# Stores of the split mixer weights on the queues of the engines that make them: high parts on ACT's, low parts on GpSimd's

## The chip, the cores and the metric

One NeuronCore of a Trainium2 chip. The time is the device time of one launch in microseconds (us); smaller is better. The engines are PE (TensorE), DVE (VectorE), ACT (ScalarE), POOL (GpSimd) and SP (SyncE). [...]

## The reference, cut to what matters

Two layers of a hybrid token mixer with a convolutional FFN, in fp32, over 512 latent tokens (`x`) and 256 context tokens (`ctx`), model width 1024:

```python
for l in range(DEPTH):                        # DEPTH = 2
    m_lat = split((silu(c) @ w_mod[l] + b_mod[l])[:, None, :], 6)
    m_ctx = split(silu(c_ctx) @ w_mod[l] + b_mod[l], 6)
    h_lat, h_ctx = modulate(x, m_lat[0], m_lat[1]), modulate(ctx, m_ctx[0], m_ctx[1])
    y_lat, y_ctx = token_mixer(h_lat, h_ctx, w_in[l], ..., w_out[l])
    x = layer_norm(ALPHA * x + m_lat[2] * y_lat, ...)
    f_lat = conv_ffn(modulate(x, m_lat[3], m_lat[4]), w_up[l], conv_w[l], w_down[l])
    x = layer_norm(ALPHA * x + m_lat[5] * f_lat, ...)
    if l == 0:                                # the same for ctx
        ...
def conv_ffn(h, w_up, conv_w, w_down, ...):
    u = conv3x3(h @ w_up)                     # 2 * 2816 columns, depthwise 3x3
    a, g = split(u, 2)
    return (silu(g) * a) @ w_down
```

## The kernel before, in words

**Products.** Every fp32 operand of a matmul is split into a high part `hi`, rounded to fp32r, and a low part `lo = x - hi`. A product is three matmuls: high by high (L183), high by low (L184), low by high (L185). ACT makes a high part (a copy, L147 and L164), POOL the low part (a subtraction in two halves, `sub_lo`, L133).

**The stage that the change touches** is layer 0's `ffn_up`, about 346 to 730 us in the trace. It runs over 44 column tiles of `w_up`. For each, `load` takes the weights from memory (SP, L140), splits them (ACT L147, POOL L133 into `lo`), and PE multiplies them with the latent tokens (result `ul`) and the context tokens (result `uc`), 48 matmuls in all. DVE then adds the nine taps of the convolution (`acc`, L945, behind a first tap by ACT, L916 and L918), and ACT (L948) and POOL (L949) finish a pair of tiles with `silu(g) * a` into `gT`.

**The queue of side work.** Behind each `load`, `fill(2)` takes two units from the list `queue`, so that work for layer 1 is done beside layer 0's matmuls. There are three kinds:

- `dot` (L315 to L318): a load of 512 KB of layer 1's modulation weights `wmodT`, then one multiply-and-sum pass by DVE (L318).
- `row` (L273 to L278): a load of 512 KB (`wmodR`), then four matmuls by PE (`mg`, L277).
- `split` (L159 to L170): a load of a block of layer 1's mixer weights (ten of `w_feat` and four of `w_tokB`, 512 KB each, four of `w_tokA`, 288 KB), a high part by ACT into `sh` (L164), a low part by POOL in place (`ms`, L133), and then two stores to scratch memory: the high part (`wh_f`, `wh_a`, `wh_b`, L168) and the low part (`wl_f`, `wl_a`, `wl_b`, L169). These 36 stores are what the change touches. Their data are first read back by `load_split` (L178), from about 925 us on.

The units stand in chunks of eight: dot, dot, dot, split, split, dot, row, row. All of them work in one pool of three buffers (tag `ms`); `sh` has a single buffer. So the first load of a chunk needs a buffer that the second split of the chunk before it gives back, which is when its low store has landed; and the second split's ACT pass needs the first split's high store to have landed.

**Order.** A scheduler arranges the instructions of each engine from the program and its own estimate of times. Before, both stores were issued by SP, in one stream with the loads of `w_up`, `wmodT`, `wmodR` and the mixer weights.

Of the kernel before, what the change touches and what calls it, by code (L numbers as in the profile page):

```python
# [58 lines left out]
def kernel(  # L59
# [22 lines left out]
    nc = tc.nc  # L82
# [39 lines left out]
    def hcol(k, t, n=1):  # L122
        if t < 4:
            a = slice(t * 128, (t + n) * 128)
            return hl[k][:, a], ll[k][:, a]
        a = slice((t - 4) * 128, (t - 4 + n) * 128)
        return hc[k][:, a], lc[k][:, a]

    def f(ap):
        return ap.bitcast(F32)  # L130

    def sub_lo(eng, lo, src, hi):
        eng.tensor_tensor(out=lo, in0=src, in1=f(hi), op=ALU.subtract)  # L133
# [23 lines left out]
    def split_units(srcs, ms):  # L157

        def step(key, src, n):  # L159
            st = ms.tile([128, 1024], F32, tag="ms", name="ms")  # L160
            hi = ms.tile([128, 1024], F32R, tag="sh", name="sh", bufs=1)
            d = [dram.tile([128, n], F32, name=f"w{p}_{key[0]}{key[1]}") for p in "hl"]
            nc.sync.dma_start(out=st[:, :n], in_=src)
            S.activation(out=hi[:, :n], in_=st[:, :n], func=AF.Copy)  # L164
            lo = st.bitcast(F32R)
            for a, b in ((0, n // 2), (n // 2, n)):
                sub_lo(G, lo[:, a:b], st[:, a:b], hi[:, a:b])
            nc.sync.dma_start(out=d[0], in_=f(hi[:, :n]))  # L168
            nc.sync.dma_start(out=d[1], in_=st[:, :n])  # L169
            split[key] = d  # L170

        return [lambda x=x: step(*x) for x in srcs]
# [914 lines left out]
    with tc.tile_pool(name="msA", bufs=2) as ms:  # L1087
        with tc.tile_pool(name="in0", bufs=1) as work, tc.tile_pool(name="ms0", bufs=5) as work_ms:
# [25 lines left out]
            for k in range(KT):  # L1114
# [5 lines left out]
                for v, (t0, n) in enumerate(((0, 4), (4, 2))):  # L1120
# [3 lines left out]
                    hi, lo = hcol(k, t0, n)  # L1124
# [169 lines left out]
```

## Time and profile before

| | |
|---|---|
| median of 3 runs | 1513.44 us (1511.74 to 1513.91) |
| the profiled execution | 1510.28 us |
| its span (first to last instruction) | 1508.5 us, so 1.78 us lie around it |
| mean granted clock of PE | 0.989 of full speed |
| busy: PE, DVE, POOL, ACT | 1448.1, 1172.2, 830.0, 544.7 us |

Busy time is an average over stages with different limits; the prediction reads the stage of the change by itself. In the trace "SPq" is SP's stream of DMA issues, "idle before, releaser" names what ended an engine's wait, and the chain of waits follows the work that ended last backwards, from each step to what released it.

### The profile page before, as it was taken

Reading aid. Unit: us, or ns where it says so; the run is one execution under the profiler, and the core shown is the slowest. Engines: PE = TensorE matmul, PEld = TensorE weight load, DVE = VectorE, ACT = ScalarE, POOL = GpSimd, SP = SyncE. Lnnn points to the kernel's source line nnn. Section 1 sums busy time; section 2 is a strip of 40 time slices with the busy share of each in tenths; the row PEclk is TensorE's granted clock in tenths of the full one; section 3 lists DMA queues with packets and bytes.
Section 4 is the critical chain, followed back from the end, with each engine's and each line's share of the span. In section 5 each row is a group of like instructions: output and inputs, shape, how many; then the busy total and the mean of one; then the engine's idle time right before and its main releaser. Section 6 shows DMA issues by size and latency. Waiting matters only on the chain.

```text
span 1508.5 us, 22357 instructions
## 1 busy us (share of the span) xinstructions
PE 1448.1 (96%) x8389; PEld 1185.7 (79%) x8389; DVE 1172.2 (78%) x1896; ACT 544.7 (36%) x936; POOL 830.0 (55%) x695
## 2 busy tenths in 40 slices
PE   6999999999999989999999989999899999999997
PEld 5776567788788878888888767986678888888875
DVE  6429987796988888787533699798687999889596
ACT  5443224245333322323211234254426454443121
POOL 2432635455665655543445597215466888777374
PEclk9999999999999999999999999999999999999999
DMA  9544410634877666521432366632162333333431
GB/s 377 195 165 158 140 54 15 228 135 159 313 266 240 239 215 216 178 70 56 165 100 85 116 204 239 209 125 71 58 234 72 98 98 98 98 98 93 173 112 56
DMA packets 67196, 227.11 MB, mean 151 GB/s; under 512 B 7289, under 2 KB 7945, under 8 KB 66065
## 3 DMA queue, kind: packets, MB, share of 16 engines
q1 hardware_dynamic: 67088, 225.69, 44.3%
q8 instruction: 66, 1.08, 0.3%
q14 instruction: 42, 0.34, 0.1%
HBM read 198.12 MB, written 27.55 MB: 150 GB/s over the span
## 4 chain that ended last, share of the span: by engine, by line
PE 62%; DVE 14%; DMA 12%; POOL 6%; issue 4%; ACT 2%; SPq 1%; POOLq 0%; DVEq 0%; ACTq 0%
PE ul L183 8%; PE ul L184 8%; PE ul L185 8%; PE f L187 5%; PE f L188 5%; PE f L189 5%; DMA ms<-in_wmodT 3%; POOL lo L133 2%; PE fl L183 2%; PE fl L185 2%; PE fl L184 2%; DVE acc L730 2%; DMA wl_f<-ms 2%; POOL ms L133 2%; PE tk L187 2%
## 5 line engine op out<-in xcount | busy, mean ns | idle before, releaser
L133 POOL TENSOR_TENSOR lo<-st,hi 128x512 fp32r<-128x512 f32 x300 | 412.2, 1397 | 228.0 <-ACT hi L147 175.1
L945 DVE SCALAR_TENSOR_TENSOR acc<-ul,cvw,acc 128x441 f32<-128x441 f32 (+2 forms) x660 | 437.1, 690 | 43.4 <-ACT acc L916 20.6
L147 ACT ACTIVATE hi<-st 128x1024 fp32r<-128x1024 f32 (+1 forms) x176 | 184.6, 1051 | 366.1 <-PE f L189 164.1
L184 PE MATMUL ul<-ll,hi 128*128 128x512 f32 (+1 forms) x768 | 286.4, 374 | 0.7 <-POOL ll L133 0.4
L183 PE MATMUL ul<-hl,hi 128*128 128x512 f32 (+1 forms) x768 | 284.8, 375 | 1.1 <-ACT hl L369 1.1
L185 PE MATMUL ul<-hl,lo 128*128 128x512 f32 (+1 forms) x768 | 285.4, 373 | 0.0
L187 PE MATMUL f<-hi,gh 128*128 128x512 f32 x440 | 171.8, 395 | 1.2 <-DVE gh L1007 1.2
L188 PE MATMUL f<-lo,gh 128*128 128x512 f32 x440 | 172.6, 394 | 0.0
L189 PE MATMUL f<-hi,gl 128*128 128x512 f32 x440 | 164.3, 396 | 6.4 <-POOL gl L133 5.3
L183 PEld LDWEIGHTS ul<-hl,hi 128*128 128x128 f32 x768 | 144.5, 190 | 28.3 <-issue 2.5
L185 PEld LDWEIGHTS ul<-hl,lo 128*128 128x128 f32 x768 | 145.5, 189 | 25.7 <-issue 0.4
L184 PEld LDWEIGHTS ul<-ll,hi 128*128 128x128 f32 x768 | 145.7, 190 | 24.6 <-POOL ll L133 0.7
L949 POOL TENSOR_TENSOR gT<-acc 128x768 f32<-128x768 f32 (+1 forms) x44 | 69.8, 1586 | 96.1 <-ACT acc L948 76.0
L730 DVE SCALAR_TENSOR_TENSOR acc<-cy,cmw,acc 128x798 f32<-128x798 f32 (+1 forms) x120 | 117.0, 1016 | 0.8
L183 PE MATMUL uc<-hc,hi 128*128 128x256 f32 x352 | 100.6, 286 | 6.5 <-DVE acc L945 6.4
L189 PEld LDWEIGHTS f<-hi,gl 128*128 128x128 f32 x440 | 82.6, 189 | 27.1 <-POOL gl L133 7.7
L185 PE MATMUL uc<-hc,lo 128*128 128x256 f32 x352 | 100.4, 285 | 0.0
L184 PE MATMUL uc<-lc,hi 128*128 128x256 f32 x352 | 100.4, 285 | 0.0
L187 PEld LDWEIGHTS f<-hi,gh 128*128 128x128 f32 x440 | 83.3, 189 | 20.6 <-issue 1.8
L188 PEld LDWEIGHTS f<-lo,gh 128*128 128x128 f32 x440 | 83.2, 189 | 18.3
L1007 DVE CAST gh<-gT 128x256 fp32r<-128x256 f32 x66 | 37.4, 572 | 64.9 <-PE f L188 64.9
L133 POOL TENSOR_TENSOR gl<-gT,gh 128x256 fp32r<-128x256 f32 x66 | 54.8, 833 | 57.8 <-DVE gh L1007 50.7
(304 smaller groups left out, 2843.6 us busy)
## 6 DMA issues: line engine op xcount, KB each, us to landing
st<-in_w_up SPq DMA_DIRECT2D x88, 512.0 KB, 3.5
st<-in_w_down SPq DMA_DIRECT2D x66, 512.0 KB, 3.5
ms<-in_wmodR SPq DMA_DIRECT2D x48, 512.0 KB, 4.1
ms<-in_wmodT SPq DMA_DIRECT2D x32, 512.0 KB, 3.7
ms<-in_wmod SPq DMA_DIRECT2D x8, 1024.0 KB, 12.3
st<-in_w_out SPq DMA_DIRECT2D x16, 512.0 KB, 3.5
x<-z SPq DMA_DIRECT2D x16, 512.0 KB, 2.8
z<-x SPq DMA_DIRECT2D x14, 512.0 KB, 8.8
```

The source lines that it names most:

```text
L133: eng.tensor_tensor(out=lo, in0=src, in1=f(hi), op=ALU.subtract)
L147: S.activation(out=hi[:, :n], in_=st[:, :n], func=AF.Copy)
L183: PE.matmul(ps, wh, xh, start=first, stop=False)
L184: PE.matmul(ps, wh, xl, start=False, stop=False)
L185: PE.matmul(ps, wl, xh, start=False, stop=last)
L187: PE.matmul(ps, xh, wh, start=first, stop=False)
L188: PE.matmul(ps, xh, wl, start=False, stop=False)
L189: PE.matmul(ps, xl, wh, start=False, stop=last)
L730: V.scalar_tensor_tensor(out=acc[i][:, :cw], in0=src, scalar=wj, in1=acc[i][:, :cw], op0=ALU.mult, op1=ALU.add)
L945: V.scalar_tensor_tensor(out=d, in0=u, scalar=w, in1=d, op0=ALU.mult, op1=ALU.add)
L949: G.tensor_tensor(out=gT[i][:, :n], in0=ag[:, :n], in1=aa[:, :n], op=ALU.mult)
L1007: V.tensor_copy(out=gh, in_=src)
```

## The change

The two stores of a split unit are issued by other engines. The high part's store goes from SP to ACT, the engine that made the high part; the low part's store goes from SP to GpSimd, the engine that made the low part. Nothing else differs; a blank line moves the lines behind 167 up by one.

```diff
             for a, b in ((0, n // 2), (n // 2, n)):
                 sub_lo(G, lo[:, a:b], st[:, a:b], hi[:, a:b])
-            nc.sync.dma_start(out=d[0], in_=f(hi[:, :n]))
-            nc.sync.dma_start(out=d[1], in_=st[:, :n])
+
+            nc.scalar.dma_start(out=d[0], in_=f(hi[:, :n]))
+            nc.gpsimd.dma_start(out=d[1], in_=st[:, :n])
             split[key] = d
```

What the scheduler makes of it is shown at three places. The first is POOL in the second chunk (near 403 us in the trace), where `ms` is the low part of a split unit, `lo` that of a tile of `w_up`, and `gT` the product that ends a pair of tiles. Before, with both stores on SP:

```order
L133 TENSOR_TENSOR ms<-ms,sh 128x512 x2
L133 TENSOR_TENSOR lo<-st,hi 128x512 x2
L133 TENSOR_TENSOR ms<-ms,sh 128x512 x2
L949 TENSOR_TENSOR gT_3372<-acc 128x768
L133 TENSOR_TENSOR lo<-st,hi 128x512 x4
```

And now:

```order
L133 TENSOR_TENSOR ms<-ms,sh 128x512 x2
L133 TENSOR_TENSOR lo<-st,hi 128x512 x2
L170 DMA wl_f_3906<-ms 128x1024
L133 TENSOR_TENSOR ms<-ms,sh 128x512 x2
L950 TENSOR_TENSOR gT_3372<-acc 128x768
L170 DMA wl_f_4001<-ms 128x1024
L133 TENSOR_TENSOR lo<-st,hi 128x512 x4
```

The stores of both split units now stand behind another POOL operation: the first behind two `lo`, the second, which ends the chunk, behind a `gT`.

The second place is POOL from the end of the fifth chunk to the sixth (about 489 to 528 us). Before:

```order
L133 TENSOR_TENSOR ms<-ms,sh 128x512 x4
L133 TENSOR_TENSOR lo<-st,hi 128x512 x2
L949 TENSOR_TENSOR gT_3378<-acc 128x768
L133 TENSOR_TENSOR lo<-st,hi 128x512 x4
L133 TENSOR_TENSOR ms<-ms,sh 128x288 x2
L949 TENSOR_TENSOR gT_3379<-acc 128x768
L133 TENSOR_TENSOR lo<-st,hi 128x512 x2
L133 TENSOR_TENSOR ms<-ms,sh 128x288 x2
```

And now:

```order
L170 DMA wl_f_4897<-ms 128x1024
L133 TENSOR_TENSOR ms<-ms,sh 128x512 x2
L133 TENSOR_TENSOR lo<-st,hi 128x512 x2
L170 DMA wl_f_4992<-ms 128x1024
L950 TENSOR_TENSOR gT_3378<-acc 128x768
L133 TENSOR_TENSOR lo<-st,hi 128x512 x4
L133 TENSOR_TENSOR ms<-ms,sh 128x288 x2
L950 TENSOR_TENSOR gT_3379<-acc 128x768
L170 DMA wl_a_5225<-ms 128x576
L133 TENSOR_TENSOR lo<-st,hi 128x512 x2
L133 TENSOR_TENSOR ms<-ms,sh 128x288 x2
L170 DMA wl_a_5320<-ms 128x576
```

The store that ends the fifth chunk (`wl_f_4992`) stands behind two `lo`, the first of the sixth (`wl_a_5225`) behind a `gT`, and the one that ends the sixth (`wl_a_5320`) directly behind its own subtraction.

The third place is SP in the sixth chunk (about 516 to 534 us). Before:

```order
L163 DMA ms<-in_w_tokA 128x576
L168 DMA wh_a_5224<-sh 128x576
L163 DMA ms<-in_w_tokA 128x576
L317 DMA ms<-in_wmodT 128x1024
L169 DMA wl_a_5225<-ms 128x576
L168 DMA wh_a_5319<-sh 128x576
L275 DMA ms<-in_wmodR 128x1024
L140 DMA st<-in_w_up 128x1024
L275 DMA ms<-in_wmodR 128x1024
L169 DMA wl_a_5320<-ms 128x576
L317 DMA ms<-in_wmodT 128x1024
```

And now:

```order
L163 DMA ms<-in_w_tokA 128x576 x2
L318 DMA ms<-in_wmodT 128x1024
L276 DMA ms<-in_wmodR 128x1024 x2
L140 DMA st<-in_w_up 128x1024
L318 DMA ms<-in_wmodT 128x1024
```

SP's stream keeps its loads, nearly in their old order, and no longer holds a store between them. Over the whole program 11 of the 18 low stores stand directly behind their own subtraction on POOL, and 7 behind a `gT` or two `lo`.

## Rows read from the trace of the kernel before

**Rows 1.** Busy time by stretch: us, PE, PEld, DVE, ACT, POOL, PEclk, DMA, GB/s.

```profile
380.00:390.00 10.00, 8.16 (x65) 6.68 (x58) 10.00 (x19) 2.11 (x3) 3.72 (x4) 1.00 0.94 328
...
530.00:552.00 22.00, 17.28 (x103) 14.45 (x102) 16.98 (x28) 4.80 (x8) 8.31 (x6) 0.92 0.53 174
...
576.00:730.00 154.00, 154.00 (x912) 135.31 (x911) 124.99 (x208) 50.67 (x73) 78.34 (x57) 1.00 0.37 120
348.00:730.00 382.00, 374.25 (x2254) 326.61 (x2253) 314.65 (x519) 128.23 (x189) 205.53 (x150) 0.99 0.58 194
```

**Rows 2.** Waits of PE, 350 to 660 us: total, times, longest.

```profile
PE uc L183 <- DVE acc L945: 6.4, 4, 4.0
PE mg L277 <- DMA ms<-in_wmodR: 0.6, 1, 0.6
```

**Rows 3.** The chain of waits, 400 to 580 us: start, us, what.

```profile
406.48 4.93 DMA wl_f<-ms
...
424.08 5.05 DMA wh_f<-sh
...
434.10 8.32 DMA wl_f<-ms
...
455.00 6.80 DMA wh_f<-sh
...
465.63 4.80 DMA wl_f<-ms
...
487.34 4.96 DMA wh_f<-sh
...
496.12 5.92 DMA wl_f<-ms
...
528.01 5.85 DMA wl_a<-ms
533.87 3.38 DMA ms<-in_wmodT
...
537.39 2.00 DVE ms L318 x2
...
548.94 2.77 DMA ms<-in_w_tokA
...
563.94 3.31 DMA wl_a<-ms
...
571.65 1.23 DVE ms L318 x2
...
574.01 0.35 PE uc L183
```

**Rows 4.** Waits in SP's stream, 350 to 660 us: total, times, longest.

```profile
SPq L168 <- ACT sh L164: 25.0, 12, 4.3
SPq L317 <- DMA wl_f<-ms: 17.3, 5, 7.9
...
SPq L169 <- POOL ms L133: 16.9, 14, 2.2
```

**Rows 5.** Timeline of SP's stream near 430 us: start, duration, instruction.

```profile
430.75 0.38 SPq L140 DMA_DIRECT2D st<-in_w_up  x1
432.79 0.81 SPq L275 DMA_DIRECT2D ms<-in_wmodR  x2
```

**Rows 6.** Timeline of POOL near 520 us: start, duration, instruction.

```profile
519.57 1.58 POOL L133 TENSOR_TENSOR ms<-ms,sh 128x288 fp32r<-128x288 f32 x2 [11.55 <-ACT sh L164]
521.11 1.84 POOL L949 TENSOR_TENSOR gT<-acc 128x768 f32<-128x768 f32 x1
522.91 2.55 POOL L133 TENSOR_TENSOR lo<-st,hi 128x512 fp32r<-128x512 f32 x2
```

**Rows 7.** DMA issues of two lines on SP: ns min/median/max, first and last start.

```profile
L169 SPq DMA_DIRECT2D wl_f<-ms x10: 326/326/962, 375.5 to 496.1; - x10
L140 SPq DMA_DIRECT2D st<-in_w_up x88: 327/328/1230, 278.9 to 1342.2; - x88
```

## The prediction

> **What bounds the kernel now.** I read the busy time by stretch first, since the change touches one stage only. PE is busy for 374.25 of the 382 us from 348 to 730 us [rows 1], so no more than 7.75 us of PE's idle time is there to be won. From 576 us on it is busy without a gap, 154.00 of 154.00 us: what happens to the side work after that reaches nobody. So only the stretch before 576 us can gain, and the whole stage can lose.
>
> Next, what PE waits for. Five waits hold nearly all of that idle time: four for DVE's taps, 6.4 us together, one of them 4.0 us, and one of 0.6 us for a load of `wmodR` [rows 2]. From 530 to 552 us PE was also granted only 0.92 of its clock [rows 1], which on 17.28 busy us cost about 17.28 x 0.08 = 1.4 us. So 6.4 + 0.6 + 1.4 = 8.4 us is the most that the change can take away.
>
> Then the chain of waits, to see why DVE is late [rows 3]. It is a loop through the three `ms` buffers. The low store that ends a chunk has to land (528.01 + 5.85 = 533.86 us); at 533.87 the next chunk's first `wmodT` load can start; it takes 3.38 us; DVE's pass over it follows, at 537.39; then more loads, the load of the split (548.94), ACT's and POOL's passes, and the next chunk's low store at 563.94. The loop ends at PE: a DVE pass at 571.65, then taps, and `uc` at 574.01. A store's landing is thus on the path although nobody reads what it wrote until far later. Three high stores are on it too (424.08, 455.00, 487.34), since `sh` has one buffer. Whatever moves these landings moves the loop, and from about 533 us on PE follows it.
>
> Last, SP's stream. It stands 25.0 us for ACT's high parts and 16.9 us for POOL's low parts, 26 times in all, and 17.3 us before `wmodT` loads that need a low store's landing [rows 4]. Loads behind a standing store are late, but the loads that the loop needs wait for a buffer anyway; the third kind of wait is the loop itself and stays.
>
> **The change part by part.** I work out how much earlier or later the sixth chunk's low store lands (before: 563.94 + 3.31 = 567.25 us), since PE's last gap follows that.
>
> First, the removed issues. SP loses 36 issues of about 0.33 us [rows 7], some 12 us, and 25.0 + 16.9 = 41.9 us of standing. SP is not on the loop by itself, so I count nothing for it; if the loop had no other limit, a load of `w_tokA` or `w_up` would go some 3 us earlier, and that stays on the side of a gain.
>
> Second, low stores that POOL's order makes late. Of the stores that end a chunk, `wl_f_4001` now stands behind a `gT` and `wl_f_4992` behind two `lo`; those take 1.84 and 2.55 us [rows 6]. Together 4.4 us on the loop. The others (`wl_f_3906`, `wl_a_5225`) end no chunk; their POOL work goes on beside them, and the second of them costs only where its buffer is wanted first by a `row` unit. On ACT, high store `wh_a_5224` moves behind two other passes, but POOL, busy with `gT` and `lo` until 522.91 + 2.55 = 525.46 us, takes the next subtraction only then: nothing.
>
> Third, the issue itself on POOL. The trace has no DMA issued by POOL. An issue on SP takes 0.33 us and counts in the landing time already, so the lower bound is nothing more; the longest on SP is 1.23 us [rows 7], and counting all of it on top is the upper bound: 0 to 1.23 us. I take 1.23 - 0.33 = 0.9 us, as a queue that is used once in some 16 us is nearer to the long issue than to the many that follow one another. Six chunk-ending stores carry it: 6 x 0.9 = 5.4 us (0 to 7.4). The first store of a chunk falls into POOL's idle time ahead of the next subtraction (11.55 us of it in rows 6), so it adds nothing; without that cover six more would add 5.4 us. ACT's issues, one per high store, lie in ACT's idle time, as ACT is busy for 128.23 of 382 us [rows 1].
>
> Fourth, relief in the queue. A store on SP lands behind the loads that SP issued before it. The low store at 434.10 took 8.32 us [rows 3]; one of `w_up` and two of `wmodR` had gone out from 430.75 us on [rows 5]. The one at 563.94, with little ahead, took 3.31. Over 3.31 us, the chunk-ending low stores at 406.48, 434.10, 465.63, 496.12 and 528.01 hold 1.6 + 5.0 + 1.5 + 2.6 + 2.5 = 13.2 us, and the high stores at 424.08, 455.00 and 487.34 hold 1.7 + 3.5 + 1.7 = 6.9 us. From another queue a store need not stand behind them. But at the best rate of these rows, 328 GB/s [rows 1], each block of 512 KB holds the DMA engines for 1.6 us whatever queue it is in; and the loads that are overtaken end later, with the loop's next load behind them in SP's queue. So the relief lies between nothing and 20.1 us, and I take half, 10.1.
>
> The Trainium skill, page "DMA: Bandwidth & Descriptors", section "Issuing engines are not separate DMA queues", says that DMAs of several engines run on the same 16 DMA engines and that issuing from several saves only the time to initiate them. The row of 8.32 us against 3.31 shows that the place in the queue also costs; by that rule the relief would be nothing, and the sum 4.4 + 5.4 = +9.8 us.
>
> The sum: 4.4 + 5.4 - 10.1 = -0.3 us. PE's gaps near 533, 545 and 574 us follow it one to one. The profiled execution has 1508.5 + 1.78 us around the span = 1510.28, so the changed kernel's would be 1510.0; that execution lies 3.16 us under the median 1513.44, and against the median the forecast is 1513.1 us. A difference of about 0.2%, 3.0 us, is what a measurement of this kernel can tell from no change.
>
> **The rivals.**
>
> *Faster: the queue was the loop's limit.* The relief comes in whole or nearly, as the overtaken loads have slack, and POOL's issue costs no more than SP's. With half the relief and no extra for the issue: 4.4 - 10.1 = -5.7 us, 1507.7 us; with all of it the cap of 8.4 us, 1505.0 us. For it speaks the row of 8.32 us; against it, that the DMA engines move 328 GB/s with a share of 0.94 in the stretch from 380 to 390 us. It decides where the relief passes 4.4 + 5.4 + 3.0 = 12.8 us at my price of an issue.
>
> *Slower: the low store has to pass POOL's stream.* POOL's issue takes the long value and the overtaken loads return what the lows gained, so that the high stores' half, 3.4 us, alone remains: 4.4 + 7.4 - 3.4 = +8.4 us, 1521.8 us. For it speak the two places in the order and that the loop ends at the low store, so a delay is added in every chunk; against it, that DVE waits for a load only in part of its passes, so that some chunks absorb a delay. It decides where the relief is below 9.8 - 3.0 = 6.8 us. The high stores on ACT are no part of it.
>
> *Slower: DVE holds up POOL's stores.* A store that POOL issues would have to wait until the DVE pass under way ends. DVE is busy 314.65 of 382 us, and a pass that it runs in the loop takes from 1.23 to 2.00 us for two instructions [rows 1, 3]; half of the mean 1.6 us, times 0.82, is 0.66 us per store, 4.0 us over six: -0.3 + 4.0 = +3.7, 1517.1 us. No row of before shows POOL issuing anything, so neither for nor against. The Trainium skill, page "SBUF — State Buffer", section "SBUF: two separate sides", warns of this: the descriptors of a DMA from GpSimd's queue are written by GpSimd's cores, which DVE locks out while it runs certain operations from SBUF to SBUF; it advises ACT's or SP's queue for it. No run here shows it yet.
>
> *No effect: the loop moves, PE doesn't.* PE has four waits for taps in the whole stretch [rows 2], so in most chunks DVE is ahead of it; if the loop shifts by less than that lead, PE ends at the same time. That lands with my forecast within 3 us.
>
> **How the numbers follow.** My forecast, with the no-effect case, gets 0.44: the terms cancel, and each has ends far apart. The faster rival gets 0.26, the POOL stream 0.20, DVE holding up the stores 0.10. So faster 0.26, same 0.44, slower 0.30. The likeliest time is 1513.1 us; its own range is 1510.1 to 1516.1. For 8 in 10 the range reaches into both sides: down to 1508.0, which takes in the faster rival to nearly its half-relief end, and up to 1521.5, which takes in DVE's case and nearly the whole of the POOL stream's.
>
> **What would show each step right or wrong.** If the relief is real, the low stores of `w_feat` land in about 3 to 6 us each with none over 7, and the first `wmodT` load of the chunk after the one at 434 us starts sooner after its subtraction than the 8.3 us of before. If POOL's order costs, `wl_f_4001` and `wl_f_4992` are issued some 2 us and 2.5 us after their subtractions. If the issue is dear, POOL's rows show a DMA instruction or a gap of about 1 us between neighbours that had none. PE's waits for DVE's taps should stay near 6.4 us in all; over 10 us would speak for the slower rivals, under 3 for the faster. SP's waits at lines 168 and 169 must be gone. The prediction is wrong if PE's gaps change by more than 3 us, above all if they change where no store of the split is near.

## The result, and the profile after

The changed kernel takes 1518.78 us (median of 20 runs, 1508.19 to 1529.88), the kernel before, run beside it, 1511.28 us (20 runs, 1508.5 to 1515.56). The ratio is 1.0053, with a 95% interval of 1.0035 to 1.0071: slower by 8.0 us (5.3 to 10.7); the medians lie 7.5 us apart. The forecast was -0.3 us, no change. The runs also scatter over 22 us, those of before over 7 us. Two single runs far above all others, of 2027.67 us (the kernel before, beside e0) and of 7402.42 us (e14b), are left out of every comparison.

The profiled execution took 1517.11 us, with a span of 1515.2 us against 1508.5. Busy time by stretch, columns as in [rows 1]:

```profile
380.00:390.00 10.00, 4.09 (x15) 2.39 (x15) 10.00 (x17) 0.00 (x0) 1.30 (x2) 0.59 0.78 274
...
530.00:552.00 22.00, 19.24 (x111) 16.46 (x110) 18.75 (x25) 6.62 (x10) 15.86 (x12) 1.00 0.63 212
...
348.00:730.00 382.00, 367.84 (x2218) 320.51 (x2219) 320.19 (x514) 129.22 (x190) 212.36 (x167) 0.98 0.56 193
```

From 348 to 730 us PE is busy for 367.84 us instead of 374.25: 6.4 us less, nearly all of the 6.7 us by which the span grew. The stretch from 530 to 552 us got better (19.24 busy us for 17.28), the one from 380 to 390 us much worse: 4.09 for 8.16, with a mean granted clock of 0.59 (1.0 is 2.4 GHz, 0.5 is 1.2 GHz) after PE had stood. PE's waits from 350 to 660 us, against [rows 2]:

```profile
PE mg L278 <- DMA ms<-in_wmodR: 9.0, 2, 8.4
PE uc L184 <- DVE acc L946: 3.0, 3, 1.8
PE gaT L327 <- DVE modT L298: 1.1, 1, 1.1
```

The waits for taps, on which the forecast had looked, fell from 6.4 to 3.0 us (two later profiles of the same kernel have 5.9 and 12.5 us, so they don't stay put). A wait of 8.4 us for a `wmodR` load came instead, and it can be followed back. Here are four timelines of the changed kernel (start, duration, instruction; in brackets the idle time before it): PE, SP, DVE and POOL.

```profile
385.91 1.08 PE L278 MATMUL mg<-ms,scT 128*32 128x256 f32 x8 [8.45 <-DMA ms<-in_wmodR]
```

```profile
381.90 0.33 SPq L276 DMA_DIRECT2D ms<-in_wmodR  x1
```

```profile
372.81 9.05 DVE L319 SCALAR_TENSOR_TENSOR ms<-ms,scB 128x1024 f32<-128x1024 f32 x1 [1.69 <-DMA ms<-in_wmodT]
381.80 0.08 DVE L319 DVE_READ_ACCUMULATOR ms<-ms,scB 128x1 f32 x1
```

```profile
372.53 0.77 POOL L170 DMA_DIRECT2D wl_f<-ms  x1 [0.31 <-POOL ms L133]
373.32 2.55 POOL L133 TENSOR_TENSOR lo<-st,hi 128x512 fp32r<-128x512 f32 x2
375.84 2.50 POOL L133 TENSOR_TENSOR ms<-ms,sh 128x512 fp32r<-128x512 f32 x2
378.31 2.47 POOL L133 TENSOR_TENSOR lo<-st,hi 128x512 fp32r<-128x512 f32 x2
380.73 0.57 POOL L170 DMA_DIRECT2D wl_f<-ms  x1
```

The `wmodR` load goes out at 381.90 us, when DVE's pass over a `wmodT` block gives its buffer back at 381.88. That pass took 9.05 us. All 32 passes, before and after (ns min/median/max):

```profile
L318 DVE SCALAR_TENSOR_TENSOR ms<-ms,scB x32: 1209/1322/2793, 362.8 to 609.6; 128x1024 f32<-128x1024 f32 x32
```

```profile
L319 DVE SCALAR_TENSOR_TENSOR ms<-ms,scB x32: 1207/1274/9055, 361.3 to 613.5; 128x1024 f32<-128x1024 f32 x32
```

So an undisturbed pass takes 1.2 us, and before none took over 2.79. The long one began while POOL issued a low store. POOL then ran six subtractions without a pause, up to the next store's issue, and the pass ended 1.1 us behind the last of them, about the length of an undisturbed pass. Only one other of the 32 took over 3 us, 5.14 us at 529.81.

The stores themselves: their issues, against [rows 7] (ns min/median/max, first and last start), and then KB each and the median us to landing:

```profile
L170 POOL DMA_DIRECT2D wl_f<-ms x10: 571/594/767, 372.5 to 501.3; - x10
```

```profile
wl_f<-ms POOLq DMA_DIRECT2D x10, 512.0 KB, 5.1
```

An issue takes POOL 0.56 to 0.77 us over all 18 low stores. SP's waits at the two store lines are gone, as the diff says. In all these runs DMAs are issued by SP, ACT and POOL alone.

### The profile page after: what moved, and what is told of

Its sections match the earlier page's. It is cut to its first block, busy times and chain, and to the rows that moved or that the text cites. A ratio compares the mean times of both kernels' runs of the same rounds, so it can differ in the third digit from the quotient of the medians.

```text
span 1515.2 us, 22354 instructions
## 1 busy us (share of the span) xinstructions
PE 1447.9 (96%) x8389; PEld 1186.1 (78%) x8389; DVE 1181.0 (78%) x1896; ACT 546.3 (36%) x936; POOL 841.4 (56%) x713
## 4 chain that ended last, share of the span: by engine, by line
PE 68%; DVE 16%; DMA 7%; POOL 4%; issue 3%; ACT 1%; SPq 0%; POOLq 0%; DVEq 0%; ACTq 0%
PE ul L184 9%; PE ul L185 9%; PE ul L186 9%; PE f L188 5%; PE f L189 5%; PE f L190 5%; DVE acc L731 2%; PE fl L184 2%; PE uc L186 2%; DVE acc L946 2%; PE uc L184 2%; PE uc L185 2%; PE fl L186 2%; PE fl L185 2%; POOL lo L133 2%
## 5 line engine op out<-in xcount | busy, mean ns | idle before, releaser
L184 PEld LDWEIGHTS ul<-hl,hi 128*128 128x128 f32 x768 | 143.7, 189 | 28.4 <-issue 2.5
```

The costliest lines, as they stand in the source:

```text
L184: PE.matmul(ps, wh, xh, start=first, stop=False)
```

## The experiments

Two theories stood against each other. **L:** once POOL issues DMAs, its operations keep DVE's operations with two SBUF inputs out for several of them (a pass reads `ms` and `scB`, both in SBUF; "long" is a pass over 3 us). **O:** the stores stand late in POOL's order, return their buffers late, and PE waits. Some expectations say **P** for a wider form of L: a DMA on POOL costs by itself, through long passes or through its own landing. Each ratio below is to the kernel before, run on the same chip.

**Highs alone to ACT** (e1).

```diff
-            nc.sync.dma_start(out=d[0], in_=f(hi[:, :n]))
+            nc.scalar.dma_start(out=d[0], in_=f(hi[:, :n]))
```

> Only the high stores move, to ACT; the low stores stay on SP, so POOL issues no DMA. Theory L (lockout: once POOL issues DMAs, its back-to-back subtractions keep DVE's two-input pass out for several of them; 9.05 and 5.14 us in the profile of the change against at most 2.79 before): no pass of DVE over 3 us, no wait of PE for wmodR over 1 us, time between 5 us under before and 1 us over it. Theory O (the loss is the stores' places in the loop: landings come late and PE waits for DVE's taps): the high stores sit directly behind ACT's pass and gain, so a gain here too, 1 to 5 us; this run alone does not separate the two, it shows what the high half gives.

Measured: 1508.92 us, ratio 0.9981 (0.9970 to 0.9993): 2.9 us faster. The longest pass takes 2.87 us. This is the fastest version that was found.

**Lows alone to GpSimd** (e2).

```diff
-            nc.sync.dma_start(out=d[1], in_=st[:, :n])
+            nc.gpsimd.dma_start(out=d[1], in_=st[:, :n])
```

> Only the low stores move, to GpSimd; the high stores stay on SP. Theory L: the whole loss is here, 4 to 12 us over before, with one to four DVE passes over 4 us, and runs that scatter by 10 us and more as those of the change do (1508 to 1530). Theory O: a loss of about 5 us with little scatter, made of many waits for taps of 1 to 4 us each, and DVE passes under 3 us.

Measured: 1518.06 us (1513.54 to 1529.12), ratio 1.0049 (1.0030 to 1.0068). The whole loss is in this half, with the scatter (16 us). Passes of 4.90, 3.27 and 3.14 us are in its profile.

**Both to ACT** (e3): as e1, and the low store by `nc.scalar.dma_start`.

> Both stores go to ACT; the stores leave SP as in the change, but POOL issues none. Theory L: no DVE pass over 3 us, runs within 6 us of each other as before, time between 6 us under before and equal. Theory O: the low stores wait in ACT's stream for their turn, as they did in POOL's, and the loss of the change stays, 3 to 8 us.

Measured: 1510.78 us, ratio 0.9987 (0.9973 to 1.0000). Leaving SP costs the low stores nothing that can be told; leaving it for GpSimd does. On average the stores don't land sooner. DMA issues before (first two rows), and with both on ACT (last two): KB each, median us to landing (of those whose landing the trace tells), 350 to 640 us.

```profile
wh_f<-sh SPq DMA_DIRECT2D x10, 512.0 KB, 5.0
wl_f<-ms SPq DMA_DIRECT2D x10, 512.0 KB, 5.5
```

```profile
wh_f<-sh ACTq DMA_DIRECT2D x10, 512.0 KB, 5.6
wl_f<-ms ACTq DMA_DIRECT2D x10, 512.0 KB, 5.9
```

**First chunk's four stores back on SP** (e7), and **only the first chunk's two lows on GpSimd** (e8).

```diff
+            q = key[0] == "f" and key[1] < 2
-            nc.sync.dma_start(out=d[1], in_=st[:, :n])
+            (nc.sync if q else nc.gpsimd).dma_start(out=d[1], in_=st[:, :n])    # e7; highs alike
+            (nc.gpsimd if q else nc.sync).dma_start(out=d[1], in_=st[:, :n])    # e8; highs on SP
```

> The change, but with the four stores of the first chunk (w_feat 0 and 1) on SP as before; the other 32 as in the change. Theory L: POOL has issued no DMA when the pass near 373 us runs, so that takes about 2 us, PE's wait of 8.4 us for wmodR is gone, and the profile's span falls by 4 to 8 us against the change's 1515.2; a long pass may still come later, so the median lies 0 to 6 us over before. Theory O: the late stores of the other chunks stay, 5 to 8 us over before, as the change.

> The kernel before, with only the two low stores of the first chunk issued by POOL, all 34 others on SP. Theory P: the pass near 373 us can be kept out as in the change (9.05 us there), 0 to 8 us over before with a wide scatter. Theory O: of the late stores only the first chunk's second (behind two lo, 2.4 us) is left; it holds the wmodR load of that chunk, 0 to 3 us over before.

Measured: e7 1516.72 us (1510.99 to 1527.12), ratio 1.0043 (1.0023 to 1.0063); e8 1511.34 us, ratio 0.9998 (0.9987 to 1.0010). In e7 the pass in the first chunk takes 1.74 us and the 8.4 us wait is gone, but the time is the change's within the intervals. A pass of 5.17 us stands at 530 us, as in the change (5.14 us there). So the first chunk's long pass isn't needed for a loss; but 2.8 us of what this profile has over before were lost by 190 us, ahead of all stores (more under e14a). In e8 the store that ends the first chunk is issued 2.44 us after its subtraction, as in the change, and nothing is lost: a late store in that place alone costs nothing that can be told.

**The change again** (e0), and **a third profile of it** (look1): the same kernel as the change.

> The change again, for a second profile beside the first. Time 5 to 10 us over before, as on record. Theory O: PE waits again for wmodR behind late low stores (near 413 us) and for taps, in the same places. Theory P: which waits there are differs from the first profile, with the passes that POOL keeps out, and the 8.4 us wait is there only if the pass near 373 us is over 4 us.

> One more profile of the change. The two profiles so far: 1517.1 us with passes 7.9 and 3.9 us longer than the shortest, and 1512.4 us with one 4.0 us longer. Theory L: the time rises with the sum of such extensions that PE ends up waiting for; a profile near 1520 us or over holds at least two of them. Theory O: the time does not follow them.

Measured: e0 1520.26 us (1511.05 to 1524.69, 12 runs), ratio 1.0050 (1.0032 to 1.0068); its profiled run took 1512.38 us and has one long pass, 5.17 us, and no wait of PE over 2.5 us. The third profile took 1519.02 us. It has passes of 5.15 and 8.62 us, and the second shows as a wait of PE. DVE, POOL and PE there:

```profile
610.90 8.62 DVE L318 SCALAR_TENSOR_TENSOR ms<-ms,scB 128x1024 f32<-128x1024 f32 x1 [3.95 <-DMA ms<-in_wmodT]
```

```profile
610.32 2.55 POOL L133 TENSOR_TENSOR ms<-ms,sh 128x512 fp32r<-128x512 f32 x2
612.83 2.52 POOL L133 TENSOR_TENSOR lo<-st,hi 128x512 fp32r<-128x512 f32 x2
615.31 0.57 POOL L169 DMA_DIRECT2D wl_b<-ms  x1
615.90 2.53 POOL L133 TENSOR_TENSOR lo<-st,hi 128x512 fp32r<-128x512 f32 x2
```

```profile
624.32 0.55 PE L183 MATMUL uc<-hc,hi 128*128 128x256 f32 x1 [6.50 <-DVE acc L945]
```

The pass lasts until POOL's run ends (618.43), and a shortest pass more. With the 8.4 us of the first profile that makes two waits of PE that follow from long passes; the run of 1512.38 us has none of that size. One long pass recurs: where the sixth chunk's subtractions run (523 to 530 us), it took 5.14, 5.17 and 5.15 us in the three profiles of the change and 5.17 in e7; in the profile of before the pass there took 1.84.

**An extra small store by POOL** (e5: one value of each partition; e11: 128 values of one partition), and **a filler without a DMA** (e6). The two big stores stay on SP.

```diff
             nc.sync.dma_start(out=d[1], in_=st[:, :n])
+            tn = dram.tile([128, 1], F32, ...); nc.gpsimd.dma_start(out=tn, in_=st[:, :1])       # e5
+            tn = dram.tile([1, 128], F32, ...); nc.gpsimd.dma_start(out=tn, in_=st[:1, :128])    # e11
+            fl = ms.tile([128, 512], F32, tag="fl", bufs=1); G.memset(fl, 0.0)                   # e6
```

> The kernel before, both stores on SP, plus one extra store of 512 bytes (one value per partition) issued by POOL behind each of the 18 split units. No store of the kernel leaves SP, so no landing and no queue of the change is there; only POOL's DMA issues are. Theory L: passes of DVE over 3 us appear again, one to four in the profile, and the median rises by 3 to 9 us with a scatter of 10 us or more. Theory O (places and landings of the stores): passes stay under 3 us and the time rises by at most POOL's own issue time on the loop, about 6 x 0.58 = 3.5 us, with the small scatter of before.

> The kernel before, both stores on SP, plus one extra store of 512 bytes of a single partition by POOL behind each split unit, instead of one value from each of 128 partitions, which took 8.5 to 12 us to land. POOL's issue is there, a slow landing is not. Theory P by DVE's long passes: one to four passes over 3 us in the profile and 3 to 8 us over before, with a scatter of 10 us. Theory O: SP's big low store lands later than the small one in nearly every unit, so nothing is late: within 3 us of before.

> The kernel before, plus a POOL memset of 128 x 512 values into a tile of its own behind each of the 18 split units: POOL's time as with a DMA issue (about 0.5 us each), but no DMA. Theory L: no DVE pass over 3 us and a time within 3 us of before. Theory O, if POOL's time is what costs: the same rise as with the small stores.

Measured: e5 1597.63 us, ratio 1.0576 (1.0552 to 1.0599); e11 1517.06 us, ratio 1.0041 (1.0026 to 1.0056); e6 1511.06 us, ratio 1.0001 (0.9989 to 1.0013). Half a microsecond of POOL's time in each unit costs nothing. In e5 neither theory had the size: the small stores land late and so should hold the buffers, and the others land late too. The DMA issues of e5 (first three rows) and the small store of e11 (last):

```profile
ms<-in_wmodR SPq DMA_DIRECT2D x15, 512.0 KB, 10.0
...
wl_f<-ms SPq DMA_DIRECT2D x10, 512.0 KB, 11.7
...
tnf<-ms POOLq DMA_DIRECT2D x10, 0.5 KB, 12.0
```

```profile
tnf<-ms POOLq DMA_DIRECT2D x10, 0.5 KB, 5.5
```

In e11 the big low stores land in 5.8 us (median), so a small one should hold its buffer no longer than the big one beside it, and the loss is there, with one long pass and, behind its taps, a wait of PE (DVE, then PE):

```profile
526.96 6.67 DVE L320 SCALAR_TENSOR_TENSOR ms<-ms,scB 128x1024 f32<-128x1024 f32 x1 [0.68 <-DMA ms<-in_wmodT]
```

```profile
539.33 0.55 PE L185 MATMUL uc<-hc,hi 128*128 128x256 f32 x1 [5.62 <-DVE acc L947]
```

The wide scatter that theory L expected did not come: e11's runs lie within 6 us of each other.

**A DMA by POOL that nobody waits for** (e14a), against **the same without the DMA** (e14b).

```diff
             nc.sync.dma_start(out=d[1], in_=st[:, :n])
+            fl = ms.tile([128, 8], F32, tag="fl", name="fl", bufs=4)
+            G.tensor_copy(out=fl, in_=st[:, :8])
+            tn = dram.tile([1, 8], F32, ...); nc.gpsimd.dma_start(out=tn, in_=fl[:1])            # e14a alone
```

> The kernel before, both stores on SP. Behind each split unit POOL copies 8 columns of the tile into a small tile of its own and issues a DMA of 32 bytes from that. The DMA holds no buffer that anything waits for; only its issue on POOL is added. Theory L: at least one DVE pass extended by over 3 us, and 3 to 7 us over the run that has the copy alone. Theory O: within 2 us of that run.

> As the run beside it, without the DMA: the copy of 8 columns alone, behind each split unit. Both theories: no DVE pass extended by over 3 us, within 2 us of before.

Measured: e14a 1516.19 us, ratio 1.0038 (1.0023 to 1.0053); e14b 1510.91 us, ratio 1.0003 (0.9990 to 1.0016). The program with eighteen DMAs of 32 bytes that hold nothing is 0.35%, 5.3 us, slower. But the profile of e14a shows no long pass:

```profile
L322 DVE SCALAR_TENSOR_TENSOR ms<-ms,scB x32: 1208/1576/2789, 365.7 to 615.9; 128x1024 f32<-128x1024 f32 x32
```

And most of the difference between the two profiles (spans of 1514.9 and 1510.8 us) was there before POOL issued anything. The same ACT operation of the token mixer, in e14b and in e14a:

```profile
188.98 0.38 ACT L777 ACTIVATE r<-tk 128x256 f32<-128x256 f32 x1
```

```profile
192.25 0.38 ACT L779 ACTIVATE r<-tk 128x256 f32<-128x256 f32 x1
```

That is 3.3 of the 4.1 us, while POOL's first DMA starts at 378.3 us. PE was granted 0.77 of its clock from 130 to 145 us in e14a, 0.89 in e14b. The profiles of e7 and e12b are late by as much at this place (192.24 and 192.68 us, against 189.43 before), those of the change by 1.4 us at most. Whether this belongs to these programs or to single executions can't be told from one profile each. So this pair doesn't show that a DMA on POOL costs 5.3 us in the stage.

**POOL's places without POOL's DMA** (e13): both stores on ACT; a copy of 8 columns by POOL, for which the low store waits, stands in POOL's order much as the DMA did (five of 18 behind two `lo` or a `gT`).

```diff
+            G.tensor_copy(out=st[:, :8], in_=st[:, :8])
+            nc.scalar.dma_start(out=d[1], in_=st[:, :n])
```

> Both stores issued by ACT, and ahead of each low store POOL copies 8 columns of the tile onto themselves. The low store waits for this copy, which stands in POOL's stream almost where the change's DMA stands (five of 18 behind two lo or a gT), so the stores are late as in the change, but POOL issues no DMA. Theory O: 4 to 8 us over before. Theory L: within 2 us of the run with both stores on ACT, that is between 4 us under before and 2 us over it, and no DVE pass over 3 us.

Measured: 1512.92 us, ratio 1.0013 (1.0001 to 1.0024), 0.26% or 3.9 us over e3 (2.1 us by the medians, and the two intervals just fail to meet), with PE's waits for taps at 10.4 us. Late places seem to cost something, but the time over before, 0.13%, is less than theory O said; the longest pass takes 2.31 us. The late stores of its profile are only in part those of the change.

**POOL's order set by hand** (e10): the change, with the later `lo` and `gT` operations behind the last low store.

```diff
+            w = nc.gpsimd.dma_start(out=d[1], in_=st[:, :n])
+            last[0] = w.ins if hasattr(w, "ins") else w
...
+    def behind_low():
+        return tc.issue_after(last[0]) if last[0] is not None else nullcontext()
...
+            with behind_low():
+                G.tensor_tensor(out=gT[i][:, :n], in0=ag[:, :n], in1=aa[:, :n], op=ALU.mult)
```

> The change, with POOL's stream ordered by hand: the low parts of w_up tiles and the gT products that come later in the program stand behind the last low store, so that each low store stands directly behind its own subtraction (in the profile of the change 7 of 18 were issued 1.7 to 2.8 us after it). Theory O (late low stores return the buffers late, and PE waits for wmodR and for DVE's taps): most of the loss goes, the time lies between 2 us under before and 3 us over it, and low stores are issued under 0.5 us after their subtraction. Theory P (a DMA on POOL costs by itself, through DVE's long passes or its own landing): the loss of 5 to 9 us stays.

Measured: 1521.41 us, ratio 1.0070 (1.0043 to 1.0097). Every low store was issued 0.3 us after its subtraction, and the loss stayed; but the order also made PE wait 2.8 us for a `lo` at 367 us, so this run doesn't clear the late places. Passes of up to 4.69 us are in it.

**DVE's pass with one SBUF input** (e9a: both stores on SP; e9b: the change), and **the short additions behind the last passes on POOL as well** (e12a, e12b). All four leave out the second 512 values of `silu(c)`.

```diff
-        S.activation(out=sc, in_=sc, func=AF.Silu)
+        sb = bank("scP", 6)
+        S.activation(out=sb, in_=sc[:, :512], func=AF.Silu)
+        sb = sb.unsqueeze(1).to_broadcast([128, 2, 512])
...
-                    rings(sm=[0, 1], big=[2, 3, 4, 5, 6], md=[7])
+                    rings(sm=[0, 1], big=[2, 3, 4, 5], md=[7])
```

> The kernel before, with the second operand of DVE's pass over wmodT in PSUM instead of SBUF, so that the pass has one SBUF input; both halves of a pass use the first 512 values of silu(c), which leaves the other 512 out, and the stage has four banks for ul instead of five. It is the base for the next run. Theory L: no pass longer than 1.5 us, also where POOL works; the time lies between 5 us under before and 3 us over it.

> The change, with the same PSUM operand (the same 512 values left out). Theory L: without a second SBUF input DVE cannot be kept out, so no pass over 1.5 us, the scatter is that of before, and the median lies within 3 us of the run with the PSUM operand and both stores on SP. Theory O: the 5 to 8 us between the change and before stay.

> The base with the PSUM operand and both stores on SP (the second 512 values of silu(c) left out), and the two short additions that follow DVE's last passes over wmodT moved to POOL, so that no DVE operation beside the split units has two SBUF inputs. Theory L and theory O alike: as the base with the PSUM operand, 3 to 9 us over before; it is what the next run is compared with.

> The change in that form (the same 512 values left out): POOL issues the low stores, but no DVE operation can be kept out. In the earlier pair 5.0 of some 9 us came from one DVE addition of 8.3 us instead of 0.6. Theory L (DVE kept out): at most 4 us over the base of this pair. Theory O (late stores and landings): 7 to 11 us over it, as in the earlier pair.

Measured: e9a 1518.33 us, ratio 1.0048 (1.0032 to 1.0064); e9b 1527.94 us, ratio 1.0115 (1.0098 to 1.0132); e12a 1516.76 us, ratio 1.0043 (1.0023 to 1.0064); e12b 1529.81 us, ratio 1.0124 (1.0105 to 1.0143). The passes all take 1.21 to 1.22 us, and the pairs still differ by 9.6 and 13.1 us: theory L expected at most 3 and 4. Of the difference between the profiles of e12a and e12b (12.7 us) 2.8 stood by about 190 us, before any store. Part of the rest is DVE again. In e9b the addition of 128 x 16 values behind the last pass, 0.18 us in e9a, was kept out (DVE, then POOL):

```profile
612.44 8.30 DVE L342 TENSOR_TENSOR modT<-modT,cst 128x16 f32<-128x16 f32 x1
620.77 0.17 DVE L343 TENSOR_SCALAR modT<-modT 128x8 f32<-128x8 f32 x1
```

```profile
612.59 2.56 POOL L133 TENSOR_TENSOR ms<-ms,sh 128x512 fp32r<-128x512 f32 x2
615.09 2.55 POOL L133 TENSOR_TENSOR lo<-st,hi 128x512 fp32r<-128x512 f32 x2
617.56 0.57 POOL L169 DMA_DIRECT2D wl_b<-ms  x1
618.16 2.54 POOL L133 TENSOR_TENSOR lo<-st,hi 128x512 fp32r<-128x512 f32 x2
```

PE waited 5.0 us for taps there. In e12b, with that addition on POOL, the next one on DVE (0.17 us in e9b, one input) took 7.07 us. Another part in e12b is PE waiting for `wmodR` twice near 380 us, 8.4 us together against 3.0 us for a buffer there in e12a: late buffers in the first chunk. So the pairs don't take theory L away as meant, and they show more of theory O than e13 does.

## Why the prediction was wrong

**The step that failed is the fourth term, the relief in the queue**, put at 10.1 us as half of 20.1. The store on which it rested, 8.32 us at 434.10 before, took 8.6 us from ACT's queue (e3) and 7.0, 7.2 and 6.9 us from GpSimd's in the three profiles of the change, so its length was hardly its place in SP's queue. The five chunk-ending low stores of the term took 29.8 us together before, from issue to landing (13.3 us over five times 3.31), and 28.4, 26.3 and 26.4 us in the change: a relief of 1.4 to 3.5 us, where half of 13.2 is 6.6. The high stores, a third of the term, landed no sooner: the median for `wh_f` is 5.0 us before, 5.8 in the change, 5.6 with both on ACT. In time, leaving SP gave 2.0 us for both stores on ACT (0 to 4.1) and 2.9 us for the highs alone. The Trainium skill, page "DMA: Bandwidth & Descriptors", section "Issuing engines are not separate DMA queues", spoke for no relief, and the median landing of the low stores, 5.5 us from SP's queue and 5.9 from ACT's, agrees with it.

With 2.0 in place of 10.1 the prediction's sum is 4.4 + 5.4 - 2.0 = +7.8 us, and 8.0 were measured. That is luck: the other two terms don't hold as they stand either.

**Late low stores (4.4 us)** were foreseen in their places: in the profile of the change seven of 18 are issued 1.74 to 2.81 us after their subtraction, as the order had shown, the others 0.30 us after. The two that the prediction priced lost 1.46 and 2.15 us against those others, 3.6 us. The late store that ends the first chunk was left out of the sum, and by e8 it costs nothing. In time, e13 over e3 gives 3.9 us (2.1 by the medians), from two sets of runs and with partly other stores late; about the size.

**The issue on POOL (5.4 us)** works on the loop with less than this. A store is issued 0.30 us after its subtraction instead of 0.03, and the issue itself counts in the landing; over six stores that makes 1.6 us.

**What the three terms come to on their own loop.** From the end of the subtraction to the landing, the five chunk-ending stores took 30.0 us before and 33.5, 31.4 and 31.5 us in the change. So the places, the issues and the relief together delayed the loop by 1.4 to 3.5 us, not by -0.3, and not by 8. What is missing is a path that the prediction didn't have: POOL keeps DVE's passes out. A pass that should take 1.23 to 2.00 us by the prediction took 9.05 us, and PE stood 8.4 us behind it.

**PE's gaps** were expected in the wrong places. They came at 377 us in one profile of the change and at 618 us in another. Both have stores of the split near, so the prediction's last sign ("where no store of the split is near") isn't met, only the size of over 3 us. But the gap at 618 us lies beyond 576 us, from where the prediction let the side work reach nobody; a long pass there used up all of PE's lead. The low store whose landing the prediction worked out (it ends the seventh chunk, not the sixth as written) landed at 567.25 us before, and at 575.4, 569.6 and 571.3 us in the change.

**The rivals.** "DVE holds up POOL's stores" had the engines the wrong way round: POOL's issues were never long, DVE's passes were. Passes over 3 us stand in eight of nine profiles of kernels in which POOL issued 14 or more DMAs in this stage and DVE's pass had both inputs in SBUF, and in none of the seven with no such DMA or two of them (2.87 at most). That PE waits for such a pass was followed in three profiles: 8.4, 6.5 and 5.6 us. The slower rival of POOL's stream was right in sign, and near in its price (8.4 us), but one of its three reasons was far off: the issue, at 7.4 us, came to 1.6. The late places and the little relief were about right.

**What is shown and what stays open.** That the loss comes from issuing the low stores from GpSimd, and not from their leaving SP, is shown by e1, e2 and e3. That long passes come with POOL's DMAs is shown by the count above; that they make up the loss is shown for single waits and argued for the whole. How the loss splits between passes kept out and late buffers stays open: the runs that were to take the first away left another DVE operation kept out, and of the 5.3 us of e14a its profile puts 3.3 us where no store is. Why POOL's DMAs should keep a pass out for several operations no run shows.

## What to carry to other kernels

Moving a store to another engine's queue frees the first engine's stream, but the store need not land any sooner; price such a gain by landings, not by the place in a queue. Before a DMA is issued from GpSimd, look at what DVE runs beside GpSimd's operations: here ACT could take the high stores (0.19% faster), GpSimd couldn't take the lows (0.49% slower). When a kernel's runs begin to scatter, look for the instruction whose longest duration has changed, not for the mean. And before a difference between two programs is put down to the line that differs, find in the traces where it arises: in e14a most of it stood ahead of that line.

## What the runs showed of the hardware

In the profile of before 19 passes of DVE, with two SBUF inputs, began while a POOL operation was under way, and 18 of them lasted until that operation's end and 1.1 us more, so they waited for one operation at most (passes up to 2.87 us against 1.2 in all profiles without POOL's DMAs). With those DMAs most passes did the same, but some were kept out for much longer: one for six POOL operations (9.05 us), an addition of 128 x 16 values took 8.30 us, and one of 128 x 8 values with a single input 7.07 us. With one operand in PSUM the pass took 1.21 to 1.22 us in all four profiles. The Trainium skill, page "SBUF — State Buffer", section "SBUF: two separate sides", describes an exclusive lock between GpSimd's operations and those of DVE that have two SBUF inputs or run in a two-port mode, held for one instruction. The passes with a PSUM operand agree with it, while a wait through six instructions is longer than it says. What that section's box warns of, GpSimd's descriptors held up by DVE, no run here shows (issues of 0.56 to 0.77 us, a median landing of 5.1 us). The other surprise was the small store: 512 bytes from 128 partitions, issued by POOL, took 12.0 us to land (median of ten), 512 bytes from one partition 5.5.
